# The low-part product of the attention scores over all 128 rows of the array, with zeros in the other component's rows

## The chip, the cores and the metric

The kernel runs on one core of a Trainium2 chip. The metric is device time in microseconds (us) of one execution, the median of several; lower is better.

## The reference, cut to what matters

One layer of a diffusion backbone works on 512 latent tokens and 256 context tokens of 1024 features: a SwiGLU block, a branch layer (attention and pooling, merged), and a second SwiGLU block, all in float32. The part that the change touches is the differential attention. Each of 8 heads has two components of 64 features, each with its own scores and softmax:

```python
def diff_attn_block(q, k, v, lam):
    s = jnp.einsum("bqhcd,bkhcd->bhcqk", q, k).astype(jnp.float32) * (HEAD_DIM ** -0.5)
    p = jax.nn.softmax(s, axis=-1)
    p = p[:, :, 0] - lam * p[:, :, 1]
    return jnp.einsum("bhqk,bkhe->bqhe", p.astype(v.dtype), v)
```

There are 512 queries and 768 keys (context before latent), so a head's scores are 2 x 512 x 768 numbers, each a sum over 64 features.

## The kernel before, in words

Activations lie transposed, features on the 128 partitions and tokens on the free dimension. A float32 product is carried by three single-pass products: both operands are split into a high part, rounded to the format float32r, and the exact rest, the low part; high x high, high x low and low x high are summed in PSUM (`mm3`, L136, L137 and L139, and the same by hand for the values, L673 to L675).

The stages follow one another: the first SwiGLU block to about 590 us, projections and attention to about 968 us, gates, pooling and merge to about 1000 us and beyond, then the second SwiGLU block and the final norm.

For the scores of a head, the two components lie on partitions 0 to 63 (`top`) and 64 to 127 (`bot`) of a projected tile. `keys` builds the tile `k` (128 x 2 x 768): for component 0 it holds the high part in the upper half of the partitions and the low part in the lower half, for component 1 the reverse. `queries` builds `q` (128 x 2 x 512), which holds the high part of a component in both halves, and `ql` (128 x 512), which holds the low parts, each component's in its own half. So for each component and each half of the keys (384 of them) two matmuls give the scores of 128 queries (`scores`): L764 multiplies all 128 rows of `q` with `k`, which sums high x high and high x low at once; L765 multiplies the 64 rows of `ql` in the component's own half with the 64 rows of `k` that hold high parts, and adds low x high.

A block is 128 queries of a head, 32 blocks in all (8 heads, `qi` 0 to 3). It issues eight such matmuls, L764 and L765 in turn, four per component, into one of two PSUM tiles `sc`. Then the softmax: the maximum (L768, VectorE), the exponential with its sum (L770, ScalarE) into a tile `e` of a pool of four, for each component; the reciprocals and the factor -lambda (L772, L773), the scaling of component 1's tile (L774, ScalarE) and the combination of both (L775, VectorE). `flip` turns the result by six transposes on TensorE (L789) and splits it, and `attend` multiplies it with the values.

What sets the order: the Python code emits the scores of a block, then independent work (projections of the next heads, from the queue of the class `Filler`, in amounts FILL_A and FILL_B), then the flip of the block before, more independent work, and every second time `attend`. Tile's planner then simulates the program with its own costs and writes down the order of each engine's instructions; something that is ready can be put ahead of earlier code that waits. A pool with several buffers under one name hands them out in turn; who gets one waits until it is free. Semaphores are generated from the dependences.

The names that the change touches: `ql` (pool `qp`, two buffers), `e` (pool `ep`, four buffers for both components), and `u` (pool `rp`, one buffer), the projection of a pooling group, which is padded by two small memsets on VectorE (L746, L747), smoothed on GpSimd, and split. Tiles named `tmp` come from `scratch`, a pool of eight.

Of the kernel before, what the change touches and what calls it, by code (L numbers as in the profile page):

```python
"""Diffusion backbone layer: macaron SwiGLU, differential attention with a context prefix, multi-scale pooling.

Activations are kept transposed (features on partitions, tokens on the free dimension), so every
product has the weights as the stationary operand. float32 products are carried by three single-pass
products of an exact split of both operands into float32r parts (high and low).
"""
# [9 lines left out]
F32 = mybir.dt.float32  # L16
F32R = mybir.dt.float32r
# [20 lines left out]
# how much independent tensor engine work goes before the scores, after each scores, after each flip, at the end  # L38
# [5 lines left out]
def shape_constants():  # L44
    """Tables that depend on shapes alone."""
    t = np.arange(SEQ)
    row, col = t // GRID_W, t % GRID_W
    half = 16
    freqs = np.float32(10000.0) ** (-np.arange(half, dtype=np.float32) / np.float32(half))
    cs = np.zeros((2, P, SEQ), np.float32)  # L50
    for d in range(P):
        pos = row if (d % 64) < 32 else col
        ang = pos.astype(np.float32) * freqs[d % 16]
        cs[0, d] = np.cos(ang)
        cs[1, d] = np.sin(ang) * np.float32(-1.0 if d % 32 < 16 else 1.0)
    edge = np.zeros((len(WINDOWS), 16), np.float32)
    for g, w in enumerate(WINDOWS):
        lo = np.clip(t - w // 2, 0, SEQ)
        hi = np.clip(t + w - w // 2, 0, SEQ)
        r = np.float32(w) / (hi - lo).astype(np.float32)  # L60
        edge[g] = np.concatenate([r[:8], r[-8:]])
    edge = np.ascontiguousarray(np.broadcast_to(edge, (P,) + edge.shape))
    return {"rope": np.ascontiguousarray(cs.transpose(1, 0, 2)), "edge": edge,
            "ident": np.eye(P, dtype=np.float32)}


class Filler:
    """Tensor engine work that can run at any time, handed out in pieces of about the asked length."""
# [17 lines left out]
    def finish(self, gen):  # L86
        """Emit everything up to and including gen."""
        while gen in self.queue:
            for _ in self.queue[0]:
                pass  # L90
            self.queue.popleft()
        self.debt = 0.0
# [3 lines left out]
def tile_layer(ctx: ExitStack, tc: tile.TileContext, a: dict, out: bass.AP):  # L96
# [20 lines left out]
    def split(hi, lo, src, lo_engine=None):  # L117
        """hi = src rounded to float32r, lo = src - hi (exact)."""
        nc.scalar.activation(out=hi, in_=src, func=AF.Copy)  # L119
        (lo_engine or nc.vector).tensor_tensor(out=lo, in0=src, in1=f32(hi), op=ALU.subtract)  # L120

    def weights(src, lo_engine=None):
        """src [128, k, n] -> (hi, lo) tiles of that shape."""
# [9 lines left out]
    def mm3(outs, wh, wl, acts, start, stop):  # L133
        """outs[i] += (wh + wl)^T (ah + al), without the product of both low parts."""
# [7 lines left out]
    # ---------------------------------------------------------------- constants and vectors  # L142
# [25 lines left out]
    def table(func, after):  # L168
        """Have the activation table of func loaded once after is there, ahead of its use."""
        nc.scalar.activation(out=dummy, in_=after[:, 0:1], func=func, scale=0.0, bias=eps)  # L170
# [10 lines left out]
    def lambdas():  # L181
        """nlam = -lambda on every partition."""
# [10 lines left out]
    # ---------------------------------------------------------------- modulations  # L193
# [5 lines left out]
    class StartMods:  # L199
        """A part of the columns of the first two modulations, in four slices, one per column group of the  # L200
        tensor engine."""
# [29 lines left out]
    class Mod:  # L231
        """One modulation: products summed over the row tiles on the vector engine, then over the rows."""
# [19 lines left out]
        def total(self):  # L252
            """Rows 32 j + 16 s on: the j-th quarter of the columns, summed over the partitions, of stream s."""
# [25 lines left out]
    def scale_vec(i, norm, kts=range(KT), ns=2):  # L279
        """g * (1 + scale), in place of the modulation with the scale."""  # L280
# [6 lines left out]
    def gate_vec(i, ns=2):  # L287
        """Half of the gate, in place."""
        t = mods[:, 8 * i:8 * i + 8, 0:ns]
        nc.vector.tensor_scalar(out=t, in0=t, scalar1=0.5, scalar2=None, op0=ALU.mult)  # L290

    # ---------------------------------------------------------------- norm over features of transposed tokens
# [8 lines left out]
    def spread(cols):  # L301
        """cols [128 tokens, n] -> PSUM [128, n * 128], the n * 128 values on every partition."""
# [6 lines left out]
    def norm_rows(acc):  # L309
        """1 / sqrt(mean + eps), the same on every partition."""  # L310
# [18 lines left out]
    class Norm:  # L329
        """adaLN of a span of tokens: the statistics, then one feature tile at a time."""  # L330
# [13 lines left out]
        def inserts(self, first):  # L344
            """Emission steps for run(): statistics after step `first`, tiles spread over the later ones."""
# [7 lines left out]
    # ---------------------------------------------------------------- token streams  # L353
# [15 lines left out]
    # ---------------------------------------------------------------- FFN  # L369
    class Hidden:  # L370
        """silu(gate) * up for 128 hidden features, split; the products come in steps."""
# [45 lines left out]
    def ffn_down(w_down, j0, acts, spans, after=no_after, held=None, lo_engine=None):  # L417
        """x += gate * (act @ w_down), one output tile per step.

        spans: (offset in act, columns, x tiles, x offset, gate modulation, stream).  # L420
        held: weights of an earlier call on the same rows, filled if empty."""
# [20 lines left out]
    def run(gen, inserts=None):  # L442
        """Exhaust gen; inserts[i] is emitted after its step i."""
# [4 lines left out]
    def ffn_chunks(w_gu, w_dn, apool, streams, spans, first, between, last):  # L448
        """Hidden features in chunks; each chunk's down product follows the next chunk's first hidden tile."""
# [13 lines left out]
    class Stats:  # L463
        """Sums of squares over features, per stream and span of tokens."""
# [9 lines left out]
    # ---------------------------------------------------------------- first FFN  # L474
# [18 lines left out]
    # sums of squares per token, one column per 128 tokens  # L493
# [29 lines left out]
    for p in range(PARTS):  # L523
# [10 lines left out]
        # units whose weights are there take this part of the features, and those before it  # L534
# [23 lines left out]
    for i in range(2, 9):  # L558
        m = Mod(i, modp, (LAT, CX) if i < 5 else (LAT,), hl[KT - 1][:, 0, 0:1].bitcast(F32) if i == 2 else None)
        # the gate of the first chunk is due early  # L560
# [35 lines left out]
    # ---------------------------------------------------------------- attention  # L596
# [12 lines left out]
    def in_unit(col):  # L609
        """Block of w_in with the 128 columns at col (those of the values lie elsewhere)."""  # L610
        return a["wi"][col // P - (V_W // P if col >= U_COL else 0), 0]

    def projection(col, streams, done, lo_engine=None):
        """Steps of a 128-column projection of each stream, then done(psum tiles)."""
# [11 lines left out]
    def rotate(src, eng):  # L626
        """Rotary embedding of a transposed projection."""
# [9 lines left out]

    def keys(hd):
        # [hi; lo] of the first component, [lo; hi] of the second
# [10 lines left out]
    def queries(hd):  # L650
        # both halves hold hi, so that one product covers hi x hi and hi x lo
        q = qp.tile([P, 2, SEQ], F32R, name="q")
        ql = qp.tile([P, SEQ], F32R, name="ql")
        qk.setdefault(hd, {}).update(q=q, ql=ql)
        off = nc.gpsimd if hd else nc.vector
        def done(i, o):
            t = rotate(o, off)
            nc.vector.tensor_scalar(out=t, in0=t, scalar1=0.125, scalar2=None, op0=ALU.mult)
            for c, own, other in ((0, top, bot), (1, bot, top)):
                split(q[own, c, :], ql[own, :], t[own], off)  # L660
# [23 lines left out]
    # the last norm of the first FFN runs while the first values are projected  # L684
# [41 lines left out]
    def pool_windows(g, u):  # L726
        """Mean over the window minus the value, in place, by sums over windows of doubling width."""
# [15 lines left out]
    def u_proj(g):  # L743
        def done(i, o):
            u = rp.tile([P, SEQ + 2 * PAD], F32, name="u")
# [8 lines left out]
    def scores(hd, qi):  # L754
        """Both components' probabilities of 128 queries, combined."""
# [4 lines left out]
        for c, own in ((0, top), (1, bot)):  # L760
            s = ps_s.tile([P, 2, 512], F32, name="sc")
            for n in range(2):
                ks = slice(n * 384, (n + 1) * 384)
                nc.tensor.matmul(out=s[:, n, 0:384], lhsT=q[:, c, qs], rhs=k[:, c, ks], start=True, stop=False)  # L764
                nc.tensor.matmul(out=s[:, n, 0:384], lhsT=ql[own, qs], rhs=k[own, c, ks], start=False, stop=True)  # L765
# [3 lines left out]
            ec = ep.tile([P, 2, 384], F32, name="e")  # L769
# [10 lines left out]
    def flip(hd, qi, prob):  # L780
        """Probabilities transposed and split."""
# [24 lines left out]
    def head_squares(hd):  # L806
        """Sums of squares of o / 256 over the head, 128 tokens per column group; they stay finite."""
# [10 lines left out]
    def head_columns(hd, rows):  # L818
        """One column per 128 tokens."""
# [4 lines left out]
    def zero_after(name, ap):  # L824
        """A zero on every partition, once ap is there."""
# [4 lines left out]
    def head_scale(h0, h1, eps_o):  # L830
        """osum -> 1 / rms; a sum that would overflow gives the zero that 1/sqrt(inf) gives."""
# [14 lines left out]
    def gate_steps(i, b, lo_engine=None):  # L846
        """The gate of branch b before its sigmoid."""
# [30 lines left out]
    # the square roots wait for the last exponential, the sigmoids for the last square root  # L878
# [8 lines left out]
    # ---------------------------------------------------------------- gates, pooling branch and merge  # L887
# [97 lines left out]
    # ---------------------------------------------------------------- second FFN and final norm  # L985
# [19 lines left out]
    class Final:  # L1005
        """Final norm of a span of tokens, turned back to natural layout tile by tile."""
# [52 lines left out]
def lay_out(v):  # L1059
    """The inputs as the kernel reads them: every block that one transfer brings lies together.  # L1060

    Weight blocks are [128 input rows, input tile, output columns]; tokens and vectors are transposed."""
    def units(w, k, n):
        # [k*128 * a, n * b] -> [b, a, 128, k, n]
# [42 lines left out]
```

## Time and profile before

| | us |
|---|---|
| median of the three runs shown | 1545.99 |
| the three runs | 1545.90, 1545.99, 1550.93 |
| span of the profiled execution, first to last instruction | 1548.4 |
| TensorE busy in it | 1520.1 |
| VectorE, ScalarE, GpSimd busy in it | 817.3, 562.1, 245.6 |

The profiled execution has no time of its own in the list beside its span. The span lies 2.4 us above the median and 2.5 us under the longest of the three runs. In the rows, PE is TensorE's matmul side and PEld its weight loads, DVE is VectorE, ACT ScalarE, POOL GpSimd, and SPq the queue that issues transfers; "idle before" in brackets is the time for which the engine did nothing ahead of an instruction, with what ended it, and "issue" there means that no other engine was waited for.

### The profile page before, as it was taken

How to read it: one execution, taken by the hardware profiler on the slowest of the kernel's cores; microseconds unless marked ns; L12 is line 12 of the kernel's file. 1: busy time of each engine (PE TensorE's matmuls, PEld its weight loads, DVE VectorE, ACT ScalarE, POOL GpSimd, SP SyncE). 2: the span in 40 equal slices, each digit the busy share in tenths (PEclk: the TensorE clock that was granted, in tenths of full speed). 3: DMA queues.
4: the chain of work that ended last, by engine and by line, in shares of the span. 5: the costliest groups of instructions: out<-in, count | busy, mean ns of one | idle time of the engine just before them, and what ended most of it. 6: DMA issues, size and time to landing. Idle time of an engine off the chain costs nothing.

```text
span 1548.4 us, 20862 instructions
## 1 busy us (share of the span) xinstructions
PE 1520.1 (98%) x8632; PEld 1284.2 (83%) x8632; DVE 817.3 (53%) x1201; ACT 562.1 (36%) x927; POOL 245.6 (16%) x191
## 2 busy tenths in 40 slices
PE   6999999999999999999999999999999999999997
PEld 4888888888888899777887777888899888888887
DVE  5767566532242259556656666633477334343446
ACT  4421221211112237455565565532256222222223
POOL 1100000000000024524454455000043000000000
PEclk9999999999999999999999999999999999999999
DMA  9454467321212123201010011332353333323221
GB/s 378 149 175 146 147 224 255 109 69 55 69 55 65 39 78 124 68 15 55 28 56 28 28 55 50 108 109 95 100 169 126 98 99 103 96 96 95 95 82 55
DMA packets 41487, 156.57 MB, mean 101 GB/s; under 512 B 4656, under 2 KB 4912, under 8 KB 37424
## 3 DMA queue, kind: packets, MB, share of 16 engines
q1 hardware_dynamic: 36640, 124.76, 24.5%
q0 software_dynamic: 4032, 29.36, 5.3%
q8 instruction: 67, 1.10, 0.3%
q10 hardware_dynamic: 720, 1.11, 0.2%
q14 instruction: 28, 0.23, 0.0%
HBM read 151.03 MB, written 4.19 MB: 100 GB/s over the span
## 4 chain that ended last, share of the span: by engine, by line
PE 94%; DVE 3%; ACT 1%; issue 1%; DMA 0%; POOL 0%; DVEq 0%; SPq 0%; POOLq 0%; ACTq 0%
PE ps L136 27%; PE ps L137 27%; PE ps L139 27%; PE sc L765 3%; PE sc L764 3%; PE ps L673 1%; PE ps L789 1%; PE ps L674 1%; PE ps L675 1%; DVE tmp L299 1%; DVE tmp L321 0%; PE acc L216 0%; PE acc L258 0%; DVE xo L437 0%; PE ps L306 0%
## 5 line engine op out<-in xcount | busy, mean ns | idle before, releaser
L119 ACT ACTIVATE w_hi<-w_raw 128x1024 fp32r<-128x1024 f32 (+1 forms) x213 | 218.2, 1026 | 757.3 <-PE ps L137 428.5
L136 PE MATMUL ps<-hl,w_hi 128*128 128x512 f32 (+1 forms) x1024 | 398.6, 392 | 0.5 <-ACT hl L119 0.3
L137 PE MATMUL ps<-hl,w_hi 128*128 128x512 f32 (+1 forms) x1024 | 393.8, 386 | 0.0
L139 PE MATMUL ps<-hl,w_lo 128*128 128x512 f32 (+1 forms) x1024 | 393.7, 386 | 0.0
L120 DVE TENSOR_TENSOR w_lo<-w_raw,w_hi 128x1024 fp32r<-128x1024 f32 (+1 forms) x175 | 205.4, 1174 | 213.0 <-ACT w_hi L119 211.6
L136 PEld LDWEIGHTS ps<-hl,w_hi 128*128 128x128 f32 x1024 | 192.4, 188 | 43.5 <-issue 5.7
L139 PEld LDWEIGHTS ps<-hl,w_lo 128*128 128x128 f32 x1024 | 192.6, 188 | 25.3 <-issue 0.7
L137 PEld LDWEIGHTS ps<-hl,w_hi 128*128 128x128 f32 x1024 | 192.9, 189 | 22.7 <-DVE hl L327 0.3
L136 PE MATMUL ps<-act_hi,w_hi 128*128 128x512 f32 (+1 forms) x592 | 200.4, 339 | 0.0
L137 PE MATMUL ps<-act_lo,w_hi 128*128 128x512 f32 (+1 forms) x592 | 192.1, 335 | 0.0
L139 PE MATMUL ps<-act_hi,w_lo 128*128 128x512 f32 (+1 forms) x592 | 175.9, 336 | 0.0
L120 POOL TENSOR_TENSOR w_lo<-w_raw,w_hi 128x1024 fp32r<-128x1024 f32 x38 | 92.8, 2443 | 518.7 <-ACT w_hi L119 474.8
L137 PE MATMUL ps<-hc,w_hi 128*128 128x256 f32 (+1 forms) x484 | 136.5, 282 | 0.0
L136 PE MATMUL ps<-hc,w_hi 128*128 128x256 f32 (+1 forms) x484 | 136.3, 283 | 0.0
L139 PE MATMUL ps<-hc,w_lo 128*128 128x256 f32 (+1 forms) x484 | 135.6, 281 | 0.0
L136 PEld LDWEIGHTS ps<-act_hi,w_hi 128*128 128x128 f32 x592 | 111.6, 189 | 19.4 <-issue 0.8
L403 DVE TENSOR_TENSOR tmp<-tmp,ps 128x512 f32<-128x512 f32 (+1 forms) x68 | 38.0, 583 | 167.5 <-PE ps L139 167.2
L437 DVE SCALAR_TENSOR_TENSOR xo<-ps,mods,xo 128x512 f32<-128x512 f32 (+1 forms) x112 | 74.9, 672 | 97.1 <-PE ps L139 96.9
L137 PEld LDWEIGHTS ps<-act_lo,w_hi 128*128 128x128 f32 x592 | 111.7, 189 | 11.9
L139 PEld LDWEIGHTS ps<-act_hi,w_lo 128*128 128x128 f32 x592 | 102.3, 190 | 5.8
L136 PEld LDWEIGHTS ps<-hc,w_hi 128*128 128x128 f32 x484 | 90.7, 188 | 17.8 <-issue 1.3
L137 PEld LDWEIGHTS ps<-hc,w_hi 128*128 128x128 f32 x484 | 91.1, 188 | 15.7 <-issue 0.2
(216 smaller groups left out, 2121.7 us busy)
## 6 DMA issues: line engine op xcount, KB each, us to landing
w_raw<-in_gu SPq DMA_DIRECT2D x88, 512.0 KB, 3.3
wm<-in_wm POOLq DMA_DIRECT2D x28, 1024.0 KB, 5.2
w_raw<-in_dn SPq DMA_DIRECT2D x40, 512.0 KB, 3.6
w_raw<-in_wi SPq DMA_DIRECT2D x36, 512.0 KB, 3.3
wm<-in_wm SPq DMA_DIRECT2D x16, 512.0 KB, 10.9
w_raw<-in_wo SPq DMA_DIRECT2D x16, 512.0 KB, 3.3
w_raw<-in_wv SPq DMA_DIRECT2D x8, 512.0 KB, 3.3
w_raw<-in_wa SPq DMA_DIRECT2D x8, 512.0 KB, 3.3
```

Of the source, the lines that this page charges most:

```text
L119: nc.scalar.activation(out=hi, in_=src, func=AF.Copy)
L120: (lo_engine or nc.vector).tensor_tensor(out=lo, in0=src, in1=f32(hi), op=ALU.subtract)
L136: nc.tensor.matmul(out=o, lhsT=wh, rhs=ah, start=start, stop=False)
L137: nc.tensor.matmul(out=o, lhsT=wh, rhs=al, start=False, stop=False)
L139: nc.tensor.matmul(out=o, lhsT=wl, rhs=ah, start=False, stop=stop)
L299: nc.vector.tensor_tensor(out=acc, in0=acc, in1=sq, op=ALU.add)
L403: nc.vector.tensor_tensor(out=g, in0=g, in1=self.ps[1][i], op=ALU.mult)
L437: nc.vector.scalar_tensor_tensor(out=xa, in0=po, scalar=mod(gate_i, i, s), in1=xa, op0=ALU.mult, op1=ALU.add)
L673: nc.tensor.matmul(out=o, lhsT=hh, rhs=vh, start=(kt == 0), stop=False)
L674: nc.tensor.matmul(out=o, lhsT=hh, rhs=vl, start=False, stop=False)
L764: nc.tensor.matmul(out=s[:, n, 0:384], lhsT=q[:, c, qs], rhs=k[:, c, ks], start=True, stop=False)
L765: nc.tensor.matmul(out=s[:, n, 0:384], lhsT=ql[own, qs], rhs=k[own, c, ks], start=False, stop=True)
```

## The change

`ql` becomes a pair of standing tiles with a plane for each component (128 x 2 x 512); the halves of the other component are set to zero once, by four memsets on GpSimd. The low part of a component is written to its own half of its own plane. L765 then multiplies all 128 rows of that plane with all 128 rows of `k`; the zero rows add nothing. Beside it, `e` is divided into two tiles for component 0 and one for component 1, and `u` becomes a `scratch` tile. Comments and docstrings were taken out, line by line; those lines are left out here.

```diff
@@ after qk, v = {}, {} @@
+    q_low = [rp.tile([P, 2, SEQ], F32R, name=f"ql{i}") for i in range(2)]
+    for t in q_low:
+        nc.gpsimd.memset(f32(t[bot, 0, :]), 0.0)
+        nc.gpsimd.memset(f32(t[top, 1, :]), 0.0)
@@ queries @@
-        ql = qp.tile([P, SEQ], F32R, name="ql")
+        ql = q_low[hd % 2]
...
-                split(q[own, c, :], ql[own, :], t[own], off)
+                split(q[own, c, :], ql[own, c, :], t[own], off)
@@ u_proj @@
-            u = rp.tile([P, SEQ + 2 * PAD], F32, name="u")
+            u = scratch(SEQ + 2 * PAD)
@@ scores @@
-        for c, own in ((0, top), (1, bot)):
+        for c in range(2):
...
-                nc.tensor.matmul(out=s[:, n, 0:384], lhsT=ql[own, qs], rhs=k[own, c, ks], start=False, stop=True)
+                nc.tensor.matmul(out=s[:, n, 0:384], lhsT=ql[:, c, qs], rhs=k[:, c, ks], start=False, stop=True)
...
-            ec = ep.tile([P, 2, 384], F32, name="e")
+            ec = ep.tile([P, 2, 384], F32, name=f"e{c}", bufs=2 - c)
```

## Rows read from the trace of the kernel before

**Rows 1.** The page: span, busy time of each engine, chain that ended last by engine.

```profile
span 1548.4 us, 20862 instructions
PE 1520.1 (98%) x8632; PEld 1284.2 (83%) x8632; DVE 817.3 (53%) x1201; ACT 562.1 (36%) x927; POOL 245.6 (16%) x191
PE 94%; DVE 3%; ACT 1%; issue 1%; DMA 0%; POOL 0%; DVEq 0%; SPq 0%; POOLq 0%; ACTq 0%
```

**Rows 2.** Attention: us, busy PE, PEld, DVE, ACT, POOL; granted clock, DMA share, GB/s.

```profile
643.00:968.00 325.00, 323.99 (x1786) 251.92 (x1787) 203.00 (x355) 189.31 (x340) 146.43 (x91) 0.98 0.12 39
```

**Rows 3.** Timeline of PE: the eight products of a block. Columns: start, us, instruction.

```profile
771.66 0.39 PE L139 MATMUL ps<-hl,w_lo 128*128 128x512 f32 x1
771.88 0.33 PE L764 MATMUL sc<-k,q 128*128 128x384 f32 x1
772.15 0.44 PE L765 MATMUL sc<-k,ql 64*128 64x384 f32 x1
...
774.36 0.43 PE L765 MATMUL sc<-k,ql 64*128 64x384 f32 x1
774.72 0.50 PE L136 MATMUL ps<-hl,w_hi 128*128 128x512 f32 x1
775.06 0.39 PE L137 MATMUL ps<-hl,w_hi 128*128 128x512 f32 x1
```

**Rows 4.** Timeline of the weight loads (PEld) at the end of the same block.

```profile
774.72 0.19 PEld L136 LDWEIGHTS ps<-hl,w_hi 128*128 128x128 f32 x1 [0.18 <-issue]
775.06 0.19 PEld L139 LDWEIGHTS ps<-hl,w_lo 128*128 128x128 f32 x1
775.29 0.19 PEld L136 LDWEIGHTS ps<-hl,w_hi 128*128 128x128 f32 x1
```

**Rows 5.** Timeline of PE: the one score product followed by a 128-row transpose.

```profile
782.94 0.34 PE L764 MATMUL sc<-k,q 128*128 128x384 f32 x1
783.12 0.39 PE L789 MATMUL ps<-ident,e 128*128 128x128 f32 x2
```

**Rows 6.** Waits of PEld, 643 to 968 us: total us, times, longest.

```profile
PEld sc L765 <- issue: 25.2, 125, 0.4
PEld sc L764 <- issue: 15.7, 84, 0.3
PEld ps L136 <- issue: 5.1, 27, 0.3
```

**Rows 7.** Timeline of POOL ahead of the attention.

```profile
600.93 1.35 POOL L120 TENSOR_TENSOR hl<-tmp,hl 128x256 fp32r<-128x256 f32 x1 [6.04 <-ACT hl L119]
```

**Rows 8.** Instructions of tile ql on POOL: ns min/median/max, first and last start.

```profile
L120 POOL TENSOR_TENSOR ql<-tmp,q x14: 1267/1296/1302, 668.5 to 924.7; 64x512 fp32r<-64x512 f32 x14
```

**Rows 9.** Timeline of ACT, DVE and PE: softmax and flip of the block of rows 3.

```profile
775.82 0.90 ACT L770 ACTIVATE e<-sc,st 128x768 f32<-128x768 f32 x1 [0.48 <-DVE st L768]
...
779.13 1.01 DVE L775 SCALAR_TENSOR_TENSOR e<-e,st 128x768 f32<-128x768 f32 x1
...
780.44 0.60 PE L789 MATMUL ps<-ident,e 128*128 128x128 f32 x4
```

**Rows 10.** Two waits of PE, and two stretches with the columns of rows 2.

```profile
643.51 0.45 PE L764 MATMUL sc<-k,q 128*128 128x384 f32 x1 [1.53 <-ACT q L661]
665.03 1.54 PE L789 MATMUL ps<-ident,e 128*128 128x128 f32 x6 [0.50 <-DVE e L775]
644.00:652.00 8.00, 8.00 (x18) 4.90 (x19) 6.03 (x10) 4.42 (x9) 4.87 (x3) 0.57 0.19 59
664.00:668.00 4.00, 3.50 (x16) 3.15 (x16) 3.14 (x8) 2.80 (x7) 0.00 (x0) 0.61 0.00 0
```

**Rows 11.** Early issues: two transfers by SP and a memset of u by DVE.

```profile
22.01 0.33 SPq L575 DMA_DIRECT2D edge<-in_edge  x1
482.58 0.43 SPq L184 DMA_DIRECT2D tmp<-in_lams  x1
591.92 0.07 DVE L746 MEMSET u<- 128x8 f32 x1
```

## The prediction

> **What bounds the kernel now.** I read the page first. TensorE is busy for 98% of a span of 1548.4 us, no other engine for more than 53%, and 94% of the chain that ended last is TensorE's [rows 1]: time that TensorE is rid of is time off the kernel, as long as the others keep up. Then the busy times by stretch: in the attention, 643 to 968 us, PE counts as busy for 324 of 325 us, but the loader of its weights for only 252, against 203 for VectorE, 189 for ScalarE and 146 for GpSimd [rows 2]. A busy PE can be a PE that waits inside an instruction, so the third view is PE's timeline. It shows the eight score products of a block from 771.88 to 774.72, 2.84 us for eight products of 384 columns [rows 3]. A 512-column product beside its like takes 0.22 to 0.23 us from start to start, with its load under the product before, one load every 0.23 us and no idle time [rows 3, 4]. The score products are shorter by a quarter and take longer: 0.36 us from L765's start to the next one's [rows 3].
>
> The weight loads tell why. Behind L765 (64 rows), the load of the next product (128 rows) comes 0.18 us after the loader came free and starts with its own product instead of ahead of it [rows 3, 4]. The waits put such idle time of the loader, for no other engine, at 25.2 us over 125 loads of L765, 15.7 over 84 of L764 and 5.1 over 27 of L136 [rows 6]. So whatever stands next to a 64-row product, on either side, loses the overlap of its load. What a 384-column product takes when its neighbour has 128 rows is shown once, where the planner put transposes behind L764: 0.18 us, from 782.94 to 783.12 [rows 5].
>
> **The change, part by part.**
>
> The products. All eight of a block become 128-row products. Now: 2.84 us, and the product after the block (774.72 to 775.06, 0.34 us) takes 0.11 more than the 0.23 of its kind, since its load was late too [rows 3, 4]; together 2.95. Then: eight at 0.18, 1.44 us [rows 5]. That is 1.51 us for a block and 32 x 1.51 = 48.3 us for all blocks. The bounds: 512-column pace scaled to 384 columns is 0.75 x 0.23 = 0.17 us a product, 8 x 0.01 x 32 = 2.6 us more, so 51; a loader that still cannot run ahead gives nothing (a rival below). A second count comes from the loader's idle time, 25.2 + 15.7 + 5.1 = 46 us in the three largest groups [rows 6]. I take 48.3, from the one row that has the very shape. The weight loads of 64 and of 128 rows both take 0.18 to 0.19 us [rows 4], so the extra rows themselves cost nothing there, and products are paced by columns [rows 3, 5].
>
> The zeros. Four memsets of 64x512 on GpSimd, once. No such memset is in the trace; the nearest row is a GpSimd write of that size with two inputs, 1.29 us [rows 8], so between 0 and 5.2 us in all. They need no data and can go as soon as their memory is free; GpSimd stands idle for 6.04 us ahead of 600.93, waiting for ScalarE [rows 7], and the first use is the score product at 643.5 [rows 10]. I take zero. If the cover is gone, the splits of `hl` behind them in GpSimd's queue come up to 5.2 us late, once, and with them the projections that read `hl`.
>
> The writes of `ql`. Same instructions, sizes and engines, into another plane. Two standing tiles alternate as two buffers did, so a head's write waits for the reads of the head two before, as now. Zero. No transfer is added, and nothing moves on SP's queue.
>
> One buffer for component 1's `e` instead of two. The exponential of a block's component 1 now waits for the combination (L775) of the block before. In the block shown the buffer is held from 775.82 to 779.13 + 1.01 = 780.14, 4.3 us [rows 9], and a block has 325 / 32 = 10.2 us now [rows 2], 8.6 after the gain. So the buffer is free before it is asked for. If it were not: ScalarE's queue stops there, and the weight splits and the evictions of the transposes behind that exponential stop with it. I take 0; a stretch of heavier softmax may cost a part of a microsecond per block.
>
> `u` as one of eight `scratch` tiles. The four pooling groups no longer wait for each other's single buffer, but take a scratch tile that rotations and squares also use. A few tenths either way; zero.
>
> What is late next. The softmax keeps its length while the tensor work around it shrinks by 1.51 us a block, and the shares of VectorE, ScalarE and GpSimd rise from 203, 189 and 146 of 325 to the same of 277 [rows 2], that is 73%, 68% and 53%. None becomes the bound, but queues get longer. The block shown has its flip 0.30 us after the combination's end (780.44 against 780.14) [rows 9]: no room, although its own scores lie wholly ahead of that interval, so the gain falls before and not in it. I charge 2 us for waits of this kind, an estimate between 0 and what the rival below takes.
>
> The sum: 48.3 - 2 = 46 us off. On the profiled execution that is 1548.4 - 46 = 1502; on the median of the runs, 2.4 us lower, 1545.99 - 46 = 1500. I predict 1500.
>
> **A rule against it.** Rows 128-wide on both sides keep the loader running ahead [rows 4]. The Trainium skill (TensorE: Matmul & The Clock Gate, Part 3: Packing small matmuls, "What overlaps and what doesn't") says that a weight load overlaps a running matmul only when the row groups differ; by it two full products never overlap their loads, and the change would give nothing. The trace disagrees: full products follow at 0.23 us, not at 0.23 + 0.19. It stays as a rival with a small chance.
>
> **The rivals.**
>
> Part of it is given back. TensorE gets through its independent work earlier and waits for the softmax at the flips. Such a wait is in the trace once, 0.50 us at 665.03, with a clock of 0.61 in the 4 us around it, against 1.0 elsewhere; 0.39 x 4 = 1.6 us more [rows 10]. The other one, 1.53 us at 643.51, is followed by 8 us at 0.57, 3.4 us lost [rows 10]. Clock and wait together are 2.1 to 4.9 us each time. One a head gives 8 x 2.1 = 17 to 8 x 4.9 = 39 us back: 1515 to 1537 with the 48.3 off. For it: the small room of rows 9. Against it: of 32 flips one waits now [rows 10], and the other engines work for 62% of the time or less [rows 2].
>
> Slower than before. The same wait in every other block: 16 x 4.9 = 78 us, 1545.99 - 48.3 + 78 = 1576. It decides from (48.3 + 8) / 4.9, that is 12 blocks of 32. The place is the flip, with the single `e` of component 1 behind it. Against it: the cycle of that buffer, 4.3 us, is half of a block's time after the change.
>
> No gain. The loads stay exposed whatever the rows: a product of 0.18 with a load of 0.19 in front is 0.37, what it is now, and the time stays at 1546. Rows 5 speak against it, and all full products.
>
> A variant on the slow side, held for less likely still: the memsets of `u` need nothing and went at 591.92, over 330 us ahead of use, as `edge` went at 22.01 [rows 11]. Were scratch tiles handed out so, four of eight would be blocked for hundreds of us. But the transfer into a scratch tile, which needs nothing either, went only at 482.58 [rows 11], its place in the code: scratch tiles come in turn.
>
> **How the numbers follow.** Forecast, 1493 to 1510: 0.83. Part given back, 1510 to 1537: 0.09. No gain: 0.03. Slower: 0.05. About 0.5%, 8 us, is what a measurement of this kernel can tell from no change; by it faster has 0.83 + 0.09 = 0.92, same 0.03, slower 0.05. For the range, the low end is 1546 - 51 and some 2 us for waits that go too, 1493; the high end takes the memsets uncovered (5) and some flips late (up to two a run of heads, 5) on top of 1500: 1510. It leaves out 0.17.
>
> **What would show it.** Right: the products L764 and L765 follow at 0.17 to 0.18 us, the product after a block starts its successor 0.23 later, the loader's "issue" idle time at the score products all but gone, the attention some 46 us shorter, other stages as they were. Wrong: score products still 0.37 apart (no gain); PE waits on L775 in many blocks with clocks around 0.6 (given back); GpSimd's memsets ahead of splits of `hl` that PE waits for.

## The result, and the profile after

The changed kernel takes 1504.49 us (median of four runs, 1504.32 to 1505.7) against 1547.29 us before; the ratio is 0.9718, with a 95% interval of 0.9703 to 0.9732. It is faster, and inside the range of 1493 to 1510, 4.5 us above the point. The profiled execution has a span of 1502.9 us in place of 1548.4, 45.5 less, and took 1504.63 us itself.

The page (compare [rows 1]):

```profile
span 1502.9 us, 20897 instructions
PE 1468.9 (98%) x8632; PEld 1280.9 (85%) x8632; DVE 813.8 (54%) x1201; ACT 559.2 (37%) x927; POOL 250.0 (17%) x195
PE 90%; DVE 5%; ACT 2%; issue 1%; POOL 1%; DMA 0%; DVEq 0%; SPq 0%; ACTq 0%; POOLq 0%
```

The same 8632 products are there and PE is busy for 51 us less; the loader's busy time has not moved (1284.2 to 1280.9). The lines are shifted: L764, L765, L770, L773, L775 and L789 of before are L769, L770, L775, L778, L780 and L794 now. The attention, with the columns of [rows 2], and the waits of PEld and of PE in it (engine, what waits, for what: total us, times, longest):

```profile
643.00:925.00 282.00, 275.67 (x1796) 250.76 (x1797) 201.69 (x360) 187.81 (x343) 149.50 (x92) 0.99 0.14 46
```
```profile
PEld ps L794 <- DVE e L780: 5.5, 2, 3.6
...
PEld sc L770 <- issue: 0.4, 2, 0.2
PEld ps L136 <- issue: 0.4, 2, 0.2
...
PEld sc L769 <- issue: 0.2, 1, 0.2
```
```profile
PE ps L794 <- DVE e L780: 4.8, 2, 3.3
...
PE sc L769 <- ACT q L666: 1.4, 1, 1.4
```

As much work passes in 282 us as in 325 [rows 2]. The loader's idle time for nothing the profile shows, 46 us in the three groups of [rows 6], is 1.0 us in the same three. In its place stands one new item, two waits at flips. PE's timeline shows both sides, in head 0's first blocks (start, us, instruction, idle time before it):

```profile
651.48 0.33 PE L769 MATMUL sc<-k,q 128*128 128x384 f32 x1
651.65 0.34 PE L770 MATMUL sc<-k,ql 128*128 128x384 f32 x1
...
652.72 0.34 PE L770 MATMUL sc<-k,ql 128*128 128x384 f32 x1
654.62 0.88 PE L794 MATMUL ps<-ident,e 128*128 128x128 f32 x6 [1.56 <-DVE e L780]
...
662.99 0.88 PE L794 MATMUL ps<-ident,e 128*128 128x128 f32 x6 [3.26 <-DVE e L780]
...
664.48 0.42 PE L680 MATMUL ps<-w_hi,hc 128*128 128x256 f32 x1
664.69 0.41 PE L678 MATMUL ps<-w_hi,hc 128*128 128x256 f32 x1
```

From the first start to the eighth are 1.24 us for seven products, 0.177 us each, against 0.36 before [rows 3]. Behind the 3.26 us wait 256-column products follow 0.21 us apart, against 0.12 elsewhere, until about 667: the lower of the clock's two levels after an idle stretch, as in [rows 10]. The kernel before had two such stretches in the attention, this one has one: behind the wait of 1.42 us at 643.89 the granted clock stayed at 1.00, where before it was 0.57 [rows 10]. Two stretches of the changed kernel, with the columns of [rows 2]:

```profile
644.00:652.00 8.00, 7.89 (x36) 6.54 (x37) 5.64 (x10) 4.82 (x9) 4.48 (x3) 1.00 0.14 41
664.00:668.00 4.00, 4.00 (x21) 4.00 (x21) 2.00 (x6) 3.91 (x9) 1.90 (x2) 0.57 0.00 2
```

Behind the attention nothing changed: the first transpose of the statistics (L306) starts at 931.4 us in place of 976.6, 45.2 earlier, and from there to the end of the span are 571.5 us, against 571.8 before.

### The profile page after: what moved, and what is told of

It reads as the page before. It is cut to its first block, busy times and chain, and to the rows that moved or that the text cites. A ratio compares the mean times of both kernels' runs of the same rounds, so it can differ in the third digit from the quotient of the medians.

```text
span 1502.9 us, 20897 instructions
## 1 busy us (share of the span) xinstructions
PE 1468.9 (98%) x8632; PEld 1280.9 (85%) x8632; DVE 813.8 (54%) x1201; ACT 559.2 (37%) x927; POOL 250.0 (17%) x195
## 4 chain that ended last, share of the span: by engine, by line
PE 90%; DVE 5%; ACT 2%; issue 1%; POOL 1%; DMA 0%; DVEq 0%; SPq 0%; ACTq 0%; POOLq 0%
PE ps L136 27%; PE ps L137 27%; PE ps L139 27%; PE sc L770 1%; PE sc L769 1%; PE ps L794 1%; PE ps L678 1%; PE ps L680 1%; PE ps L679 1%; DVE tmp L299 1%; DVE tmp L321 1%; DVE e L780 1%; DVE st L773 1%; PE acc L216 0%; ACT e L775 0%
```

## The experiments

Ratios are against runs of the kernel before on the same chip in the same session. Where a time is set beside the changed kernel's (1504.5 us in the result, 1504.9 in experiment 5), the two can come from different sessions.

**1. The low-part product back on 64 rows, all else of the change kept.**

```diff
-        for c in range(2):
+        for c, own in ((0, top), (1, bot)):
-  matmul(..., lhsT=ql[:, c, qs], rhs=k[:, c, ks], ...)
+  matmul(..., lhsT=ql[own, c, qs], rhs=k[own, c, ks], ...)
```

> The changed kernel with its low-part products back on 64 rows (the component's own half of ql and k); standing ql tiles, zeros, three tiles e and u in scratch stay. If the whole gain is the 64-row products' lost load overlap: 128 products at about 0.37 us again and the time of the kernel before, 1543 to 1551 us. If the other edits carry a part: below 1540. If the other edits cost something: above 1552.

1549.72 us (ten runs), before 1549.41, ratio 1.000 (0.999 to 1.001). The loader's idle time is back (PEld's waits, 643 to 968 us):

```profile
PEld sc L770 <- issue: 24.6, 124, 0.3
PEld sc L769 <- issue: 16.1, 86, 0.3
PEld ps L136 <- issue: 5.1, 27, 0.3
```

All of the gain needs the 128-row product. The rest of the change (zeros, standing tiles, one buffer of `e`, `u` in scratch) costs and brings nothing by itself that can be told from 0.1%, 1.5 us.

**2. Fewer changes of rows: per component two full products, then two of 64 rows** (the kernel before, reordered; the edit in short, `full` and `low64` are the products of L764 and L765).

```diff
-  for n in range(2): full(c, n); low64(c, n)
+  for n in range(2): full(c, n)
+  for n in range(2): low64(c, n)
```

> The kernel before with each component's four products in the order full, full, 64-row, 64-row. If the price is one for each change between full and 64-row products (0.39 us for entering and leaving together), half of the changes go: 32 x 4 x 0.196 = 25 us off, about 1522. If a load overlaps only a product on other rows, the two 64-row products (same rows) don't overlap either: a third of the lost starts goes less, about 12 us off, 1535. If 64-row products are slow by themselves: no change, 1547.

1527.27 us, ratio 0.9852 (0.9837 to 0.9866): half of the gain. PE's timeline, a block's last two and a half groups:

```profile
774.50 0.62 PE L767 MATMUL sc<-k,ql 64*128 64x384 f32 x2
775.05 0.62 PE L764 MATMUL sc<-k,q 128*128 128x384 f32 x2
775.60 0.62 PE L767 MATMUL sc<-k,ql 64*128 64x384 f32 x2
776.14 0.50 PE L136 MATMUL ps<-hl,w_hi 128*128 128x512 f32 x1
776.48 0.39 PE L137 MATMUL ps<-hl,w_hi 128*128 128x512 f32 x1
```

Two products of a kind take 0.55 us, where two full products beside their like take 0.36: a price of 0.19 us for each change of rows, not for each 64-row product. A block with four changes costs 8 x 0.18 + 4 x 0.19 = 2.2 us, with eight 2.96, as measured before (2.95). That is 32 x 0.76 = 24.3 us; PE waits at flips for 3.2 us in place of 0.5, and 24.3 - 2.7 = 21.6 against 22.1 between the medians.

**3. The fewest changes: four full products, then four of 64 rows on upper and lower half in turn** (in short again; the block now takes both PSUM tiles `sc` at its start).

```diff
+  for c: for n: full(c, n)
+  for n: for c, own: low64(c, n, own)
```

> The kernel before with a block's products in the order four full ones, then four 64-row ones, upper and lower half of the rows in turn. If only the change between full and 64-row products costs: 32 islands of four, 3/4 of the lost 50 us goes, about 1510. If products on different halves also run side by side, up to 2 x 0.18 us a block more goes, about 1498. If each change of rows costs like the others: 32 x 0.6 = 19 us off, about 1528.

1512.78 us, ratio 0.9765 (0.9749 to 0.9781). A whole group of four on PE's timeline:

```profile
785.70 0.86 PE L764 MATMUL sc<-k,q 128*128 128x384 f32 x4
786.49 0.62 PE L768 MATMUL sc<-k,ql 64*128 64x384 f32 x4
787.04 0.39 PE L136 MATMUL ps<-hc,w_hi 128*128 128x256 f32 x1
787.27 0.28 PE L137 MATMUL ps<-hc,w_hi 128*128 128x256 f32 x1
```

Four 64-row products and the change behind them take 0.55 us, what two took in experiment 2: on different halves two of them run side by side. The eight take 787.04 - 785.70 = 1.34 us, and the product behind them 0.23 in place of 0.12; together 1.45, as much as eight full ones (1.44): two changes more, 0.38, and two products beside others, 0.36 less. In PE's queue only 19 of the 32 blocks have the four together; the others are split into ones, twos and threes and pay for more changes. In the whole queue PE goes from 128 to 64 rows or back 256 times in the kernel before, 132 times in experiment 2, 90 times here and never in the changed kernel. So this order would draw level with the change at best, and here it does not. The Trainium skill (TensorEngine Tiling (Array Packing), Tiling Modes) says that changing the tiling mode drains TensorE, and that different tiles can run in parallel. The trace agrees with both, 0.19 us a change here.

**4. More work ahead of the two late flips.** 2.5 and 3.5 us more independent work before head 0's first two.

```diff
-  fill.run(FILL_A)
+  fill.run(FILL_A + (FIRST[qi] if hd == 0 else 0.0))
```

> The changed kernel with 2.5 and 3.5 us more independent tensor work ahead of the flips of the first two blocks of head 0. If the two waits of PE for L780 (1.56 and 3.26 us, with the clock behind the second) are what was given back: 3 to 6 us off, about 1499 to 1501. If the work is only moved and the wait comes at another flip: 1504.

A miss: 1510.69 us (1510.19 to 1512.26), 6 us more than the changed kernel. The first two flips wait no longer, but the supply of independent work is given, and it ran out at the end: PE waits for 3.2 us at 878.7 and again at 930.2, and the clock is low behind both (0.92 over 925 to 970 us). PE's waits, 643 to 968 us:

```profile
PE sc L769 <- ACT e L775: 3.6, 2, 3.2
PE ps L794 <- DVE e L780: 3.2, 1, 3.2
```

**5. The changed kernel again,** as the base for the next three.

> The changed kernel once more, beside the three that vary it: 1504 to 1506 us.

1504.91 us, ratio 0.971 (0.9696 to 0.9725), the same two waits of 4.8 us in all.

**6. The product by -lambda on ScalarE.** In the trace of after, VectorE's L778, a product of one number per partition, takes 0.16 us in 20 of the 32 blocks and 1.96 in the block of the long wait. GpSimd's row beside it ends within 0.02 us of it (660.79 and 660.81):

```profile
658.85 1.96 DVE L778 TENSOR_TENSOR st<-st,nlam 128x1 f32<-128x1 f32 x1
```
```profile
658.43 2.36 POOL L120 TENSOR_TENSOR w_lo<-w_raw,w_hi 128x1024 fp32r<-128x1024 f32 x1
```

In the other late flip it is the same, 651.24 + 1.25 = 652.49 beside a GpSimd product that ends at 652.47:

```profile
651.24 1.25 DVE L778 TENSOR_TENSOR st<-st,nlam 128x1 f32<-128x1 f32 x1
```
```profile
651.18 1.29 POOL L633 TENSOR_TENSOR tmp<-tmp 128x512 f32<-128x512 f32 x1
```

The Trainium skill (SBUF — State Buffer, "Who interferes with whom") says that a VectorE instruction with two inputs in SBUF contends with a GpSimd instruction that reads SBUF; both rows agree. L778 is longer than 0.2 us in ten other blocks too (up to 2.18 us at 689.6, each time to the end of a GpSimd instruction), and PE waits in none of them. Nor is it new: before the change the same instruction (L773) was held in 13 blocks, head 0's first one among them (1.19 us), and ScalarE waited for it without a wait of PE (ScalarE's waits before, 643 to 968 us):

```profile
ACT e L774 <- DVE st L773: 9.2, 10, 1.5
```

So a held L778 costs time only where PE has nothing else to do.

```diff
-  nc.vector.tensor_tensor(out=st[:, 6:7], in0=st[:, 5:6], in1=nlam, op=ALU.mult)
+  nc.scalar.activation(out=st[:, 6:7], in_=st[:, 5:6], func=AF.Copy, scale=nlam)
```

> The changed kernel with the factor -lambda (L778, one number per partition) multiplied on ScalarE instead of VectorE. L778 took 1.25 and 1.96 us in the two blocks whose flips PE waited for, with a split of weights running on GpSimd, and 0.16 us elsewhere. If that stretch is what made the flips late: the two waits of PE shrink from 4.8 us to below 2, and 2 to 4 us go, 1501 to 1503. If the wait is only moved on (to the combination L780, or to a later flip): 1504 to 1506.

1502.71 us (1502.33 to 1505.05), ratio 0.9702 (0.9687 to 0.9716). PE's waits, 643 to 968 us:

```profile
PE sc L769 <- ACT e L775: 1.6, 1, 1.6
...
PE ps L794 <- DVE e L780: 1.2, 2, 0.7
PE ps L137 <- DVE pa_lo L120: 1.2, 2, 1.0
PE ps L136 <- ACT pa_hi L119: 0.7, 1, 0.7
```

The flips' wait went from 4.8 to 1.2 us, but in three other groups, where results of ScalarE or VectorE are late, PE now waits for 3.5 us, against 0.7 at such places before: 0.8 us less waiting in all. The median fell by 2.2 us, with ranges that overlap; in this trace the clock did not fall behind the second flip either (1.00 over 664 to 668 us). Experiments 11 and 12 below, where the same edit is the only difference, put it at 1.5 us with ranges that just do not overlap. The expectation speaks of a split of weights beside both held instructions and of 0.16 us elsewhere: beside the first it was a product of the rotation (L633), and elsewhere it holds for 20 blocks of 30.

**7 and 8. Seven scratch tiles in place of eight, and with them a second buffer for component 1's `e`** (with eight scratch tiles the second buffer finds no room; the edit of `ec` is experiment 8's alone).

```diff
-  tmp = pool("tmp", bufs=8)
+  tmp = pool("tmp", bufs=7)
...
-  ec = ep.tile([P, 2, 384], F32, name=f"e{c}", bufs=2 - c)
+  ec = ep.tile([P, 2, 384], F32, name=f"e{c}", bufs=2)
```

> The changed kernel with seven scratch tiles instead of eight, to make room for the next one. If scratch tiles are short in the attention: slower by 1 us or more; if not: 1504 to 1506 us.

> As the one before, and component 1's exponentials get their second tile back; the order of the instructions of every engine is that of the one before. If the single tile costs nothing after the gain: the same time within 1 us. If it gives back a part: 2 us off or more, and the waits of ScalarE's exponential for L780 go.

1512.8 us with seven tiles, 1513.38 with the second buffer besides (1513.14 to 1514.13). The two do not differ by more than their ranges: one buffer for `e` is not what the flips wait for (4.7 us with two). The 8 us that both lost against experiment 5 are another matter: the attention ended 3.3 us earlier (L306 at 928.3 against 931.6 us; more products in the stages ahead of it, 2689 against 2678 from 100 to 560 us), and behind it, where PE is never idle, every stretch holds fewer products.

**9 to 12. Is it the number of tiles, or where the others lie?** An unused tile of 64 or 128 bytes per partition behind the scratch tiles moves all that lies behind them and touches no instruction of the work; for 128 bytes it is `[P, 32]`. A scratch tile has 2112 bytes, so seven tiles and 64 bytes move it by 2048.

```diff
+  pad = pool("pad", bufs=1).tile([P, 16], F32, name="pad")
+  nc.vector.memset(pad, 0.0)
```

> The changed kernel, eight scratch tiles, with an unused tile of 64 bytes per partition behind the scratch tiles, so that everything allocated behind them lies 64 bytes further on; no instruction of the work differs. If the slower pace of the 512-column products that the run with seven scratch tiles showed (0.2333 us start to start in place of 0.2267) comes from where the operands lie, by a shift of 64 beyond a multiple of 128 bytes, then it comes here too: 512-column products at 0.233 us behind the attention and about 11 us more than the changed kernel, 1515 to 1516 us. If it came from having seven scratch tiles (more waits for one), then no change: 1504.5 us and 0.2267 us.

> The same with an unused tile of 128 bytes in place of 64: the control. If the place counts by what is left over a multiple of 128 bytes: the changed kernel's time, 1504.5 us, products at 0.2267 us. If any shift from the present layout costs the pace: 1515 us and 0.233 us. If layout is not the cause: 1504.5 us as well.

> Seven scratch tiles and the unused tile of 64 bytes: what lies behind the scratch tiles is then moved by 2048 bytes against the changed kernel, a multiple of 128, while the count of scratch tiles is seven. Layout theory: the pace of the changed kernel comes back (0.2267 us), and with it the 3 us or so that the seven-tile run was ahead at the end of the attention: about 1501.5 us. Count theory: as the seven-tile run, 1512.8 us and 0.233 us.

> The run before (seven scratch tiles, 64 bytes of padding) with the product by -lambda on ScalarE: if layout explains the pace and the waits at the first two flips go down from 4.8 to about 1.2 us as they did in the run with that edit alone, about 2 us less than the run before, 1499.5 us, the shortest of all; if the count of tiles explains the pace, about 1511 us.

Medians: 64 bytes 1505.24 us (1503.69 to 1505.52), 128 bytes 1516.82 (1515.09 to 1518.44), seven tiles with 64 bytes 1504.07 (1503.4 to 1504.51), the same with -lambda on ScalarE 1502.6 (1501.56 to 1503.39, ratio 0.97, 0.9682 to 0.9718), the lowest median of all, though no lower than experiment 6 (1502.71) by more than the ranges tell. The last two lie 2.6 and 3.1 us above what was expected (1501.5 and 1499.5): with the old place half of the lead of seven tiles went too (L306 at 929.9 us, 2678 products from 100 to 560 us again). The stretches say what the medians hide. Two stretches from 960 us on, with the columns of [rows 2]: first experiment 5, then 128 bytes, then seven tiles with 64.

```profile
960.00:1000.00 40.00, 40.00 (x178) 33.14 (x177) 14.21 (x17) 12.80 (x16) 0.00 (x0) 1.00 0.36 119
1000.00:1400.00 400.00, 398.73 (x2030) 341.63 (x2029) 185.65 (x217) 132.71 (x188) 33.55 (x24) 1.00 0.34 107
```
```profile
960.00:1000.00 40.00, 40.00 (x173) 32.47 (x173) 14.72 (x17) 11.75 (x15) 0.00 (x0) 1.00 0.32 105
1000.00:1400.00 400.00, 398.70 (x1992) 334.37 (x1991) 180.53 (x212) 131.25 (x186) 33.53 (x24) 1.00 0.33 106
```
```profile
960.00:1000.00 40.00, 40.00 (x178) 33.10 (x178) 15.05 (x18) 12.09 (x16) 0.00 (x0) 1.00 0.32 103
1000.00:1400.00 400.00, 398.73 (x2030) 341.63 (x2029) 185.13 (x216) 132.10 (x187) 33.74 (x24) 1.00 0.34 108
```

PE is busy all the time at a granted clock of 1.00, and 400 us hold 2030 or 1992 products. The 512-column products follow 0.2267 us apart in the first and third and 0.233 in the second, the 256-column ones 0.12 in all three. Seven tiles alone gave 1994; seven tiles moved back by the padding give 2030 again, to the product. So it is the place and not the number of tiles. The theory of multiples of 128 bytes, though, is refuted: 128 bytes are slow where it expected 1504.5, and a shift of 2048 costs nothing, so it is not any shift either. With 64 bytes the time stays, as the theory of the number of tiles expected, but for another reason: products behind the attention are slower (173 in 40 us, 2017 in 400), while those of the first FFN are faster (2692 from 100 to 560 us, against 2678), and L306 (L308 there) starts at 925.3 us. Which operand's place counts, and by what rule, stays open.

## Why the prediction was right

**The products, 48.3 us.** Confirmed, with about 47 us measured. Experiment 1 differs from the changed kernel in that alone, and the medians by 1549.72 - 1504.91 = 44.8 us, the profiled spans by 1548.9 - 1503.1 = 45.8 us. Two things stand in this beside the products. The waits at flips, 4.8 us against 0.5, hide 4.3 us of the gain. The clock adds to it: experiment 1's trace has both low stretches of [rows 10], the changed kernel's only the second:

```profile
644.00:652.00 8.00, 8.00 (x19) 5.06 (x19) 5.93 (x10) 4.52 (x9) 4.78 (x3) 0.57 0.18 51
```

The prediction reckoned 3.4 us for the first stretch [rows 10] and had no term for losing it; taken as about 3 us, 45.8 + 4.3 - 3 leaves 47. Why the clock fell behind that wait in one kernel and not in the other is not shown. The mechanism was right as stated too, and experiments 2 and 3 make it sharper: what costs is the change between 64 and 128 rows, 0.19 us each, and not the 64-row product. The row with the transposes [rows 5] was the right one to take, 0.18 us against 0.177 measured. That loads of 64 rows take 0.18 us too, for which the prediction names rows with loads of 128 rows only, is so in the trace before.

**The zeros.** Four memsets of 0.52 us, 2.1 us in all, inside the bounds of 0 to 5.2, on GpSimd from 591.84 us:

```profile
591.84 0.52 POOL L640 MEMSET ql<- 64x512 f32 x1 [0.40 <-DVE tmp L321]
...
593.54 0.52 POOL L641 MEMSET ql<- 64x512 f32 x1
```

The first score product started at 643.89 us against 643.51 [rows 10], in an execution that was already 0.47 us late at 31 us, long before the memsets. Hidden, as charged.

**The writes of `ql`, one buffer of `e`, `u` in scratch, 0 each.** Right together by experiment 1, at the old pace of the scores. For `e`, experiment 8 shows it alone and at the new pace; ScalarE's exponential waited for the buffer once, 0.9 us.

**The late flips, 2 us.** The mechanism was right, the size too small. Two flips wait, both in head 0's first blocks, 4.8 us in all and 4.3 more than before. The prediction spread small waits over the blocks; what decided most of it was a VectorE instruction of one number per partition held for 1.25 and 1.96 us beside GpSimd, which it did not look for: 4.8 us became 1.2 without it (experiment 6).

**The sum and the median.** The sum, 46 us off the profiled execution, came out at 45.5 in the spans, and this is in part luck: about 1 us less from the products and 2.3 more at the flips than forecast stand against about 3 from the clock, which the sum left out. Of the 4.5 us on the median, 0.5 is the sum (1548.4 - 46 = 1502.4 against a span of 1502.9). The other 4 are the step from the span to the median: the prediction took 2.4 us off, but the profiled execution of the changed kernel took 1.7 us more than its span (1504.63), and each execution that is listed with both took 1.7 to 3.1 more. By that the profile before, with its span of 1548.4, is of the execution of 1550.93. In later sessions the executions of the kernel before with a mean granted clock of 0.998 took 1546.1 to 1546.6 us, those with 0.995, the clock of this profile, 1550.1 to 1551.8; so the base of 1545.99 is a time like the former, and the rows come from one like the latter.

**The rivals.** Part given back (two waits, 1.56 and 3.26 us, not one a head) happened at a quarter of its lower price (4.3 of 17 us). Slower would have needed 12 late blocks of 32; there are 2. The rival of no gain fell: full score products follow each other 0.177 us apart with their loads hidden. The sentence of the Trainium skill behind it (TensorE: Matmul & The Clock Gate, Part 3: Packing small matmuls, "What overlaps and what doesn't"), that a load overlaps only where row groups differ, does not hold for the 128-row products here; the loss came where the row groups changed.

## What to carry to other kernels

Look at PE's timeline for products that take longer than their columns, and at the loader's idle time without a releaser: a product on 64 rows between products on 128 rows costs a change going in and one coming out, and padding its operand with zeros to 128 rows is free if the product alone is paced by its columns. When TensorE gains time in one stage, look first where its independent work is thinnest: there the wait came here, and moving that work only moved the wait. Before subtracting a term from a base, see whether the profiled execution is like the one that gave the base: its clock too. Before crediting a few microseconds to an edit that changes the memory layout, look at the pace of products that the edit does not touch.

## What the runs showed of the hardware that was not expected

The pace of full products with PE never idle and the granted clock at 1.00 depends on where the tiles lie: 2030 or 1992 products in the same 400 us, about 2%, for a shift of 128 bytes. Over the whole kernel that is 12 us, a quarter of what the change brought. It has no part in that gain: the kernel before, the changed one and experiment 1 all hold 2030.

Four 64-row products, on upper and lower half in turn, took with the change behind them 0.55 us, no more than two on the same half did.
